# One-core hybrid decoder trunk: the layer norm's steps reordered on VectorE and ScalarE, its third output block staggered further, the last gate block moved to other PSUM banks, the first tile's scores put off

## The chip, the cores and the metric

One core of a Trainium2 chip runs the whole program. The metric is the device time of one execution in microseconds, as the median of several runs. TensorE (PE) does the matmuls, VectorE (DVE), ScalarE (ACT) and GpSimd (POOL) the elementwise work, and SyncE (SP) issues most DMAs. Each engine works through its own queue in order, and engines wait for one another through semaphores.

## What is computed

Two layers over a stream of 1024 positions by 1024 channels: a convolution branch and then an attention branch, each followed by a gated embedding.

```python
# layer 0
h = rms_norm(x, norm_g[0]);  a, b, gate = split(h @ w_in, 3)
y = a * sigmoid(b)
y = depthwise_conv(y, dw) + dw_b                      # 31 taps, causal
y = layer_norm(y, ln_g, ln_b)                         # over the 1024 channels
x = x + (silu(y) * silu(gate)) @ w_out
# after each layer i
gate = sigmoid(rms_norm(x, ple_norm_g[i]) @ ple_w_gate[i])
x = x + (p[i] @ ple_w_proj[i]) * gate
# layer 1
h = rms_norm(x, norm_g[1])
q, k, v, gate = split(h @ attn_w_in, ...)             # 3 dilation groups, 8 heads each, 64 wide
q, k = rope(rms_norm(q)), rope(rms_norm(k))
o = softmax-weighted sum over the groups of banded attention(q, k, v)
x = x + (o * silu(gate)) @ attn_w_out
```

## The kernel before

Channels lie on the 128 partitions, in 8 blocks n of 128; positions lie along the free dimension, in two halves h of 512. A matrix product keeps about float32 precision by splitting both operands into a high part (a rounded copy, made on ACT by `hi_of`) and a low part (the rest, made by `lo_of` on DVE or POOL); each block of products is three matmuls, high by high, high by low and low by high. `weights` (L240) queues a weight block's load, its high part and its low part; the load's target, `raw`, has two buffers.

**The order is written out by hand.** `Order.at(t, fn)` notes a step with a planned time, and `run` issues all steps sorted by it. Planned times set only the order in each engine's queue; they are not waited for. The layer norm's plan is in `Q['ln']`, counted from U, the time planned for its first step.

**The layer norm** (L609 to L676). For each half: `center` (L618) subtracts the mean, which PE has summed into PSUM, from the 8 blocks on DVE, and ACT squares them; `add` (L625) sums the squares, blocks 1 to 3 on POOL and 5 to 7 on DVE; `stat1` (L629) sums over the partitions on PE; `first1` and `step1` (L637, L640) form the reciprocal root (a table load, Ln and Exp on ACT, then four DVE steps); and for each block `yn` (multiply on DVE, SiLU on ACT), `yg` (multiply by the gate on POOL), `ya` (high part on ACT) and `yb` (low part on DVE). Beside it PE computes the last gate blocks (`gacc`, L597 to L606); `gate` multiplies such a block on DVE out of PSUM and takes SiLU on ACT, which needs another table than Ln and Exp. The low parts of the last gate weights and of the first three output weights `w_o` are in the same queues.

**The output product** (L693 to L714). Its first three blocks run together as the halves' channel blocks k become ready: `step_o(n, h, k)` is three matmuls. Blocks 0 and 1 take k at once, block 2 two steps later, and never before U + 30. The other five blocks follow one at a time, then eight embedding blocks `gacc2` (L790 to L827), each evicted by `ple`: a multiply on DVE out of PSUM (L780), a sigmoid on ACT (L781), a multiply and an add. The product's PSUM tiles come in turn from two buffers tagged `mm`; the tile `t` comes from eight buffers tagged `X`, and the result is stored by a DMA from ACT's queue.

**The start of attention** (L1303 to L1362). Attention runs over 48 tiles of 128 positions; each has 24 steps c of two projection matmuls on PE, and `STAGES` (L78) says at which step of which later tile each of a tile's other stages is issued. `turn` transposes q and k on PE, `khi` and `qhi` make their high parts on ACT, `klo` and `qlo` the low parts on DVE; `klo` also issues the DMAs that copy the key parts across partitions in `ring`; `score` is on PE, `top` on DVE, `exp` on ACT. The projected and roped `qs` has one buffer, which the square of the next tile takes as well. The first two tiles share their weights' arrival: tile 1's first half of steps runs inside tile 0, and the stages of both are held back.

Of the kernel before, what the change touches and what calls it, by code (L numbers as in the profile page):

```python
# [58 lines left out]
    rf=-0.1,  # L59

    ln=dict(
        cen=([0.62 * n for n in range(8)], [6.9, 7.5, 8.2, 9.9, 10.5, 15.6, 16.2, 16.8]),
        add=(5, 17.5),
        st=(8, 20.5),
        r1=(9.8, 22.4),
        r2=(11.6, 24.4),
        yn=([14.2, 14.9, 19.5, 20.2, 21, 23, 23.6, 27.2], [26 + 0.7 * n for n in range(8)]),
    ),
)
WKB = 18  # L70
# [17 lines left out]
    11: ((2, "score 0"), (2, "score 1"), (3, "values 0"), (2, "top 0"), (3, "cross 0"),),  # L88
    12: ((2, "top 1"), (2, "exp 0"),),
    15: ((3, "values 1"),),  # L90
    18: ((1, "turn"), (1, "qhi"), (1, "khi"),),
    19: ((3, "store 0"),),
    20: ((1, "klo"), (2, "exp 1"), (3, "cross 1"),),
    22: ((1, "qlo"), (3, "store 1"),),
# [22 lines left out]
class Order:  # L117
# [5 lines left out]
    def at(self, t, fn):  # L123
        self.ops.append((t, len(self.ops), fn))
# [8 lines left out]
def kernel(ctx: ExitStack, tc: tile.TileContext, a, out):  # L133
# [106 lines left out]
    def weights(o, wp, src, nk, t, eng=None, hi=None, lo=None):  # L240

        w = {}
        o.at(t - 30, lambda: w_dma(wp, w, src, nk))
        o.at(t - 14 if hi is None else hi, lambda: w_hi(wp, w, nk))
        o.at(t - (10 if eng is dve else 13) if lo is None else lo, lambda: w_lo(wp, w, nk, eng or pool))
        return w
# [72 lines left out]
    def mm(name):  # L319
        return ps.tile([P, S], F32, name=name, tag="mm", bufs=2)  # L320
# [273 lines left out]
    T_c += Q['mean']  # L594
    U = T_c + Q['cen']
    for n in range(KT):
        wg = weights(o, wp, a["w_cin"][16 + n], KT, T_g + C * n, (pool, dve)[Q['wge'][n]],  # L597
                     lo={5: T_g + C * n - 0.15, 6: U + 6.7, 7: U + 6.8}.get(n))
        te, gacc = chunk(o, T_g + C * n, lambda: mm("gacc"), wg, hh, hl, KT)

        def gate(n=n, gacc=gacc):
            gates[n] = G("gate")
            dve.tensor_mul(gates[n], gacc["a"], rb0)
            act.activation(gates[n], gates[n], AF.Silu)
        at(U + Q['ln']['r1'][0] + 0.05 if n == 5 else te + (0.3 if n == 7 else Q['gt']), gate)

# [32 lines left out]
        rstd_step([sv["rb"][:, halves[h]]], [sv["rt"][:, halves[h]]], [sv["xm", h]])  # L641

    L = Q['ln']
    at(U + 7.4, lambda: act.preload_act_table_set("natural_log_exp_and_others"))
    for h in range(2):
        for n in range(KT):
            at(U + L['cen'][h][n], lambda n=n, h=h: center(n, h))
            if n % 4:
                at(U + (L['add'][h] + 0.65 * (n - 5) if n > 3 else L['cen'][h][n] + 0.1), lambda n=n, h=h: add(n, h))
        at(U + L['st'][h], lambda h=h: stat1(h))  # L650
        at(U + L['r1'][h], lambda h=h: first1(h))
        at(U + L['r2'][h], lambda h=h: step1(h))
    yh, yl, ready = [None] * KT, [None] * KT, [[], []]
    tg = 0
    for h, n in [(0, n) for n in range(7)] + [(1, 0), (1, 1), (0, 7)] + [(1, n) for n in range(2, KT)]:
        def yn(n=n, h=h):
            d = dch[n][:, halves[h]]
            dve.tensor_mul(d, d, sv["rb"][:, halves[h]])
            act.activation(d, d, AF.Silu, scale=vec[:, V_LNG, n : n + 1], bias=vec[:, V_LNB, n : n + 1])

        def yg(n=n, h=h):
            d = dch[n][:, halves[h]]
            pool.tensor_mul(d, d, gates[n][:, halves[h]])

        def ya(n=n, h=h):
            if yh[n] is None:
                yh[n] = H("yhi")
            hi_of(yh[n][:, halves[h]], dch[n][:, halves[h]])

        def yb(n=n, h=h):  # L670
            if yl[n] is None:
                yl[n] = H("ylo")
            lo_of(yl[n][:, halves[h]], dch[n][:, halves[h]], yh[n][:, halves[h]])
        ty = U + L['yn'][h][n]
        tg = max(ty + 1.4, T_g + C * (n + 1) + 1.5 if n == 7 and not h else 0, tg + 1.6)
        at(ty, yn)  # L676
        at(tg, yg)
        at(tg + 1.7, ya)
        at(tg + 3.4, yb)
        ready[h].append(tg + 4.2)  # L680
# [6 lines left out]
    def reopen():  # L687
# [2 lines left out]
        late["gp"] = tc.alloc_tile_pool(name="gp2", bufs=1, side="right", reuse_waits="tile")  # L690
    at(ready[1][-1] + Q['rf'], reopen)

    w_o = [weights(o, wp, a["w_cout"][n], KT, T_o + 8 * n, (pool, dve, dve)[n], U + (9.7, 19, 28.5)[n], U + (9.95, 19.4, 29.5)[n])  # L693
           for n in range(3)]
    acc_o = [{}, {}, {}]

    def open_o():
# [7 lines left out]
                      stop=k == KT - 1 and ww is w["l"])  # L705
    at(T_o - 0.1, open_o)
    for h in range(2):
        for k in range(KT + 2):
            for n in range(3):
                kk = k - 2 if n == 2 else k  # L710
                if 0 <= kk < KT:
                    T_o = max(T_o, ready[h][kk], U + 30 if n == 2 else 0)
                    at(T_o, lambda n=n, h=h, kk=kk: step_o(n, h, kk))
                    T_o += 0.7  # L714
    for n in range(KT):
# [70 lines left out]

    h2h, h2l = [None] * KT, [None] * KT
    at(T_e + 7.5, lambda: ple_stat(lambda: half("ssb2"), X, s2))
    s3 = {}
    ends = []  # L790
    for n in range(KT):
        tn = T_e + C * n + (1.8 if n else 0)
        w = weights(o, wp, a["w_pg"][0, n], KT, tn)
        te, acc = chunk(o, tn, lambda: mm("gacc2"), w, gh, gl, KT)

        def ev1(n=n, acc=acc, what=0):
            s3["t", n] = ple(n, acc["a"], X, s2, halves if n == 7 else whole, s3.get(("t", n)), 5, what)
# [499 lines left out]
    for c in range(24 * (NT - 1) + max(place.values()) + 1):  # L1297
# [24 lines left out]
        for lag, st in STAGES.get(c % 24, ()):  # L1322
            if 0 <= i - lag < NT:
                nm, *pr = st.split()
                held.append((c if i != 1 else max(36, c) if c < 40 else c + 9, getattr(tiles[i - lag], nm), pr))
        for t, fn, pr in [h for h in held if h[0] <= c]:
            fn(*map(int, pr))
        held = [h for h in held if h[0] > c]
# [266 lines left out]
```

## Time and profile before

| | us |
|---|---|
| median of 3 runs | 1317.41 (1316.56 to 1320.78) |
| the profiled execution | 1321.62 |
| its span, first to last instruction | 1319.8 |
| PE busy | 1259.9 |
| DVE, ACT, POOL busy | 999.0, 702.1, 628.1 |

In a timeline row the first number is the start from the beginning of the span, the second the duration; rows of one kind that follow each other are merged (x2, x8). What stands in brackets is how long the engine had idled and what it had waited for. "busy" of merged matmuls includes their overlap: a matmul of 512 columns starts every 0.23 us at the full clock.

### The profile page before, as it was taken

The page shows a single profiled execution, that of the slowest core. Times are in us where ns is not written, and L with a number is a line of the kernel's source. Part 1 is how long each engine was busy: PE and PEld are TensorE (multiplying, and loading weights), DVE is VectorE, ACT ScalarE, POOL GpSimd, SP SyncE. Part 2 cuts the span into 40 slices and gives each one's busy share as a digit, 9 for nine tenths or more (in the row PEclk, how much of TensorE's full clock was granted, in tenths as well). Part 3 has the DMA queues.
Part 4 walks back from the last instruction along what each step waited for, and adds up shares of the span by engine and source line. Part 5 has one row for each costly group of instructions (what it writes and reads, how often), then busy time and mean ns, then how long its engine had stood idle before and what let it go on. Part 6 is the DMA issues. An engine that isn't in the chain of part 4 may idle for free.

```text
span 1319.8 us, 18998 instructions
## 1 busy us (share of the span) xinstructions
PE 1259.9 (95%) x6432; PEld 1043.9 (79%) x6432; DVE 999.0 (76%) x2038; ACT 702.1 (53%) x1552; POOL 628.1 (48%) x742
## 2 busy tenths in 40 slices
PE   7999899999599999899999899999999999999998
PEld 5778788877388788779888799788887888768786
DVE  6899989999948444647987977988878888764522
ACT  6555564556633334645765755655655656424411
POOL 2679899996515355022422622423324424246342
PEclk9999999999799999989999899999999999999999
DMA  7124131113114444601311311411213312117453
GB/s 282 49 99 156 48 128 33 65 32 112 47 50 154 165 176 159 201 17 41 112 61 36 114 56 25 120 25 40 58 47 96 116 30 66 53 50 269 164 203 128
DMA packets 50933, 128.13 MB, mean 97 GB/s; under 512 B 6252, under 2 KB 19764, under 8 KB 50836
## 3 DMA queue, kind: packets, MB, share of 16 engines
q1 hardware_dynamic: 47380, 114.33, 26.7%
q10 hardware_dynamic: 3456, 12.58, 2.5%
q8 instruction: 51, 0.84, 0.3%
q14 instruction: 46, 0.38, 0.1%
HBM read 84.75 MB, written 27.46 MB: 85 GB/s over the span
## 4 chain that ended last, share of the span: by engine, by line
PE 72%; DVE 10%; issue 6%; POOL 6%; ACT 4%; DMA 2%; SPq 0%; POOLq 0%; DVEq 0%; ACTq 0%
PE gacc L183 16%; PE pqk L998 14%; PE oacc L183 8%; PE pv L999 7%; PE bacc L183 5%; PE aacc L183 3%; PE pacc L358 3%; PE oacc L704 2%; POOL wkl L173 2%; PE po L1144 2%; PE tp L1058 2%; PE tq L1126 2%; DVE eA L578 1%; DVE oB L578 1%; PE gacc L1257 1%
## 5 line engine op out<-in xcount | busy, mean ns | idle before, releaser
L998 PE MATMUL pqk<-wkh,h2n 128*128 128x512 f32 x512 | 203.1, 409 | 0.0
L561 POOL TENSOR_TENSOR cc<-cc,tt 128x512 f32<-128x512 f32 x118 | 167.0, 1415 | 21.3 <-ACT tt L560 14.4
L1028 POOL TENSOR_TENSOR fh<-fh 128x8 f32<-128x8 f32 x48 | 9.9, 205 | 290.8 <-ACT fh L1024 286.4
L999 PE MATMUL pv<-wkh,h2n 128*128 128x256 f32 x512 | 144.5, 282 | 0.0
L173 POOL TENSOR_TENSOR wl<-raw,wh 128x1024 fp32r<-128x1024 f32 (+1 forms) x39 | 90.5, 2321 | 70.9 <-ACT wh L167 70.9
L560 ACT ACTIVATE tt<-eo,dws 128x512 f32<-128x512 f32 x118 | 83.4, 721 | 72.9 <-POOL cc L561 72.8
L998 PEld LDWEIGHTS pqk<-wkh,h2n 128*128 128x128 f32 x512 | 98.5, 192 | 19.0 <-issue 2.4
L1120 ACT ACTIVATE pt<-pt,stt 128x128 f32<-128x128 f32 (+1 forms) x192 | 85.1, 444 | 45.5 <-DVE stt L1112 44.0
L998 PE MATMUL pqk<-wkl,h2n 128*128 128x512 f32 x256 | 104.7, 409 | 0.0
L999 PEld LDWEIGHTS pv<-wkh,h2n 128*128 128x128 f32 x512 | 98.8, 193 | 0.0
L578 DVE SCALAR_TENSOR_TENSOR eA<-ypad,dw,eA 128x513 f32<-128x513 f32 x120 | 89.5, 746 | 0.0
L173 DVE TENSOR_TENSOR ring<-tp,ring 64x256 fp32r<-64x256 f32 x96 | 40.5, 422 | 53.7 <-ACT ring L167 50.3
L578 DVE SCALAR_TENSOR_TENSOR oB<-ypad,dw,oB 128x512 f32<-128x512 f32 x104 | 77.5, 745 | 0.0
L1150 ACT COPY ot<-po 64x128 f32<-64x128 f32 x192 | 49.1, 256 | 52.1 <-PE po L1144 50.7
L999 PE MATMUL pv<-wkl,h2n 128*128 128x256 f32 x256 | 72.1, 282 | 0.0
L781 ACT ACTIVATE pt<-pt 128x1024 f32<-128x1024 f32 (+2 forms) x19 | 17.5, 925 | 98.7 <-DVE pt L780 98.7
L167 ACT ACTIVATE wh<-raw 128x1024 fp32r<-128x1024 f32 (+1 forms) x51 | 50.9, 997 | 35.0 <-PE oacc L704 17.9
L780 DVE TENSOR_TENSOR pt<-gacc,rb 128x1024 f32<-128x1024 f32 (+2 forms) x19 | 19.9, 1055 | 64.2 <-PE gacc L183 57.7
L167 ACT ACTIVATE qq<-tp 64x256 fp32r<-64x256 f32 x96 | 36.3, 378 | 53.6 <-PE tp L1058 53.0
L173 POOL TENSOR_TENSOR wkl<-raww,wkh 128x768 fp32r<-128x768 f32 (+1 forms) x24 | 42.5, 1781 | 41.0 <-ACT wkh L167 38.2
L784 POOL TENSOR_TENSOR pt<-pt,xi 128x1024 f32<-128x1024 f32 x12 | 28.9, 2405 | 68.5 <-DVE pt L783 43.1
L1160 DVE TENSOR_TENSOR og<-po,ot 64x128 f32<-64x128 f32 x192 | 54.6, 284 | 6.0
(302 smaller groups left out, 3909.0 us busy)
## 6 DMA issues: line engine op xcount, KB each, us to landing
raww<-in_w_ain_dram SPq DMA_DIRECT2D x48, 384.0 KB
ring<-ring SPq DMA_DIRECT2D x96, 128.0 KB
raw<-in_w_cin_dram SPq DMA_DIRECT2D x22, 512.0 KB
proj_d<-pout SPq DMA_DIRECT2D x16, 512.0 KB
x_d<-x ACTq DMA_DIRECT2D x16, 512.0 KB
raw<-in_w_pg_dram SPq DMA_DIRECT2D x16, 512.0 KB
pj<-proj_d SPq DMA_DIRECT2D x16, 512.0 KB
xi<-x_d SPq DMA_DIRECT2D x16, 512.0 KB
```

Of the source, the lines that this page charges most:

```text
L167: act.activation(hi, src, AF.Copy)
L173: (eng or dve).tensor_sub(lo, src, f(hi))
L183: pe.matmul(dst, w_[:, k, :], x[k][:, sl], start=(k == 0 and i == 0 and j == 0), stop=(k == nk - 1 and i == 1))
L358: pe.matmul(acc[:, sl], q[w, k][:, c], q[x, k][:, sl], start=(k == 0 and ii == 0 and j == 0), stop=(k == 1 and ii == 1))
L560: act.activation(tt, src, AF.Copy, scale=w)
L561: pool.tensor_add(sv["c", n], sv["c", n], tt)
L578: dve.scalar_tensor_tensor(acc, src, w, acc, op0=ALU.mult, op1=ALU.add)
L998: pe.matmul(self.pqk, x, ww[:, :512], start=a0, stop=a1)
L999: pe.matmul(self.pv, x, ww[:, 512:], start=a0, stop=a1)
L1120: act.activation(x, x, AF.Exp, scale=-1.0, bias=nm, accum_out=den)
L1150: act.copy(t[h * HD : h * HD + HD], self.po[pr][HD - h * HD : P - h * HD, h, 0])
L1160: dve.tensor_add(tok(self.u.og[pr][pp[h]], self.g, self.s), *(runs(x, self.g) for x in (self.po[pr][pp[0], h, 1], self.ot[pr][pp[h]])))
```

## The change

In the layer norm, the first half's eight blocks are now finished ahead of the second half's: the second half's centring, its sums, `stat1`, `first1`, `step1` and all of its `yn` are issued later, and block 7 of the first half no longer stands between blocks of the second. The low part of gate weight 6 goes ahead of the layer norm on POOL, that of gate weight 7 from POOL to DVE; gates 5, 6 and 7 and the three output weights get other places. Output block 2 runs five steps behind blocks 0 and 1 in the first half and level with them in the second, without the bound of U + 30. The last embedding block (`gacc2`, n = 7) takes the PSUM tile `eA` in place of an `mm` buffer, and its result tile is `rb0`, which is free by then, in place of an `X` buffer. In attention `khi` is issued ahead of `qhi` for every tile, and the stages `score`, `top` and `exp` of tile 0 are issued 8 steps later.

```diff
     ln=dict(
-        cen=([0.62 * n for n in range(8)], [6.9, 7.5, 8.2, 9.9, 10.5, 15.6, 16.2, 16.8]),
-        add=(5, 17.5),
-        st=(8, 20.5),
-        r1=(9.8, 22.4),
-        r2=(11.6, 24.4),
-        yn=([14.2, 14.9, 19.5, 20.2, 21, 23, 23.6, 27.2], [26 + 0.7 * n for n in range(8)]),
+        cen=([0.62 * n for n in range(8)], [6.9, 7.5, 9.5, 17.0, 18.2, 20.6, 22.0, 23.0]),
+        add=((5, 5.65, 6.3), (23.4, 24.5, 25.1)),
+        st=(6.6, 27.5),
+        tab=7.2,
+        r1=(10.2, 29.6),
+        r2=(12.2, 31.8),
+        yn=([14.6, 15.2, 15.8, 16.4, 17.6, 20.0, 21.4, 28.2], [34.2 + 0.7 * n for n in range(8)]),
+        gate={5: 11.0, 6: 19.0, 7: 27.9},
+
+        wg={6: (-0.5, 0), 7: (8.2, 1)},
+        wo=((8.6, 9.7, 0), (22.5, 26.2, 1), (28, 30.5, 1)),
     ),
@@
-    18: ((1, "turn"), (1, "qhi"), (1, "khi"),),
+    18: ((1, "turn"), (1, "khi"), (1, "qhi"),),
@@
-        wg = weights(o, wp, a["w_cin"][16 + n], KT, T_g + C * n, (pool, dve)[Q['wge'][n]],
-                     lo={5: T_g + C * n - 0.15, 6: U + 6.7, 7: U + 6.8}.get(n))
+        lo, eng = (U + Q['ln']['wg'][n][0], Q['ln']['wg'][n][1]) if n > 5 else (U - 5 if n == 5 else None, Q['wge'][n])
+        wg = weights(o, wp, a["w_cin"][16 + n], KT, T_g + C * n, (pool, dve)[eng], lo=lo)
@@
-        at(U + Q['ln']['r1'][0] + 0.05 if n == 5 else te + (0.3 if n == 7 else Q['gt']), gate)
+        at(U + Q['ln']['gate'][n] if n > 4 else te + Q['gt'], gate)
@@
-    at(U + 7.4, lambda: act.preload_act_table_set("natural_log_exp_and_others"))
+    at(U + L['tab'], lambda: act.preload_act_table_set("natural_log_exp_and_others"))
@@
-                at(U + (L['add'][h] + 0.65 * (n - 5) if n > 3 else L['cen'][h][n] + 0.1), lambda n=n, h=h: add(n, h))
+                at(U + (L['add'][h][n - 5] if n > 3 else L['cen'][h][n] + 0.1), lambda n=n, h=h: add(n, h))
@@
-    for h, n in [(0, n) for n in range(7)] + [(1, 0), (1, 1), (0, 7)] + [(1, n) for n in range(2, KT)]:
+    for h, n in itertools.product(range(2), range(KT)):
@@
-    w_o = [weights(o, wp, a["w_cout"][n], KT, T_o + 8 * n, (pool, dve, dve)[n], U + (9.7, 19, 28.5)[n], U + (9.95, 19.4, 29.5)[n])
-           for n in range(3)]
+    w_o = [weights(o, wp, a["w_cout"][n], KT, T_o + 8 * n, (pool, dve)[e], U + hi, U + lo)
+           for n, (hi, lo, e) in enumerate(L['wo'])]
@@
-        for k in range(KT + 2):
+        lag = 0 if h else 5
+        for k in range(KT + lag):
             for n in range(3):
-                kk = k - 2 if n == 2 else k
+                kk = k - lag if n == 2 else k
                 if 0 <= kk < KT:
-                    T_o = max(T_o, ready[h][kk], U + 30 if n == 2 else 0)
+                    T_o = max(T_o, ready[h][kk])
@@
-    s3 = {}
-    ends = []
+    s3 = {("t", 7): rb0}
@@
-        te, acc = chunk(o, tn, lambda: mm("gacc2"), w, gh, gl, KT)
+        te, acc = chunk(o, tn, (lambda: mm("gacc2")) if n < 7 else (lambda: ps.tile([P, S], F32, name="gacc2b", tag="eA", bufs=1)),
+                        w, gh, gl, KT)
@@
-                held.append((c if i != 1 else max(36, c) if c < 40 else c + 9, getattr(tiles[i - lag], nm), pr))
+                held.append((c + 8 if i == lag == 2 else c if i != 1 else max(36, c) if c < 40 else c + 9, getattr(tiles[i - lag], nm), pr))
```

## Rows read from the trace of the kernel before

**Rows 1.** PE's waits over the span: us in total, times, longest.
```profile
PE tp L1058 <- POOL qs L1052: 8.8, 12, 1.4
PE sc L1097 <- DMA ring<-ring: 3.7, 2, 2.6
```

**Rows 2.** Timeline of PE in the layer norm: start, duration, instruction, [idle before].
```profile
338.86 0.40 PE L704 MATMUL oacc<-yhi,wh 128*128 128x512 f32 x1
...
356.10 0.80 PE L704 MATMUL oacc<-yhi,wh 128*128 128x512 f32 x1 [12.73 <-ACT wh L167]
...
359.05 0.80 PE L704 MATMUL oacc<-yhi,wl 128*128 128x512 f32 x1 [1.73 <-DVE wl L173]
```

**Rows 3.** Chain that ended last, in order of time: start, length, what.
```profile
359.05 31.86 PE oacc L704 x124
...
530.79 9.06 DMA x_d<-pt
...
586.78 0.95 PE sc L1097 x8
```

**Rows 4.** Stretches: length, busy time per engine, granted clock, DMA share, GB/s.
```profile
348.00:365.00 17.00, 7.17 (x16) 5.25 (x17) 17.00 (x14) 10.08 (x15) 13.61 (x8) 0.50 0.18 62
...
542.00:546.00 4.00, 4.00 (x15) 3.42 (x14) 3.36 (x6) 2.37 (x4) 0.00 (x0) 0.57 0.73 263
...
573.00:580.00 7.00, 6.29 (x21) 5.38 (x22) 2.26 (x11) 0.88 (x4) 1.46 (x4) 0.51 0.07 19
```

**Rows 5.** Timeline of DVE in the layer norm.
```profile
295.05 3.65 DVE L557 SCALAR_TENSOR_TENSOR cc<-eo,dws,cc 128x512 f32<-128x512 f32 x2 [0.66 <-POOL cc L561]
...
300.12 0.69 DVE L586 TENSOR_TENSOR d<-cc,Bs 128x512 f32<-128x512 f32 x1
...
302.93 4.88 DVE L619 SCALAR_TENSOR_TENSOR d<-mb,d 128x512 f32<-128x512 f32 x8 [0.98 <-PE mb L612]
...
308.78 4.14 DVE L627 TENSOR_TENSOR sq<-sq,sq 128x512 f32<-128x512 f32 x2 [0.38 <-ACT sq L623]
...
371.60 1.21 DVE L173 TENSOR_TENSOR w<-raw,w 128x1024 fp32r<-128x1024 f32 x1
```

**Rows 6.** Timeline of POOL in the layer norm.
```profile
294.98 2.39 POOL L173 TENSOR_TENSOR wl<-raw,wh 128x1024 fp32r<-128x1024 f32 x1
304.97 1.30 POOL L627 TENSOR_TENSOR sq<-sq 128x512 f32<-128x512 f32 x1 [7.60 <-ACT sq L623]
...
309.53 5.62 POOL L173 TENSOR_TENSOR wl<-raw,wh 128x1024 fp32r<-128x1024 f32 x2
```

**Rows 7.** Groups of POOL from 340 to 372: busy, mean ns, idle before.
```profile
L663 POOL TENSOR_TENSOR d<-d,gate 128x512 f32<-128x512 f32 x12 | 20.4, 1722 | 8.3 <-ACT d L659 5.4 <-ACT gate L604 2.8
```

**Rows 8.** Timeline of ACT at a change of tables in the layer norm.
```profile
341.17 1.28 ACT L659 ACT_TABLE_LOAD   x1
342.46 1.52 ACT L659 ACTIVATE d<-d,vec 128x512 f32<-128x512 f32 x2
```

**Rows 9.** Timeline of PE, DVE and ACT around the last embedding block.
```profile
541.38 0.47 PE L998 MATMUL pqk<-wkh,h2hi 128*128 128x512 f32 x1 [3.15 <-ACT pt L781]
...
544.69 0.84 ACT L167 ACTIVATE wkh<-raww 128x768 fp32r<-128x768 f32 x1 [1.33 <-DMA raww<-in_w_ain_dram]
...
548.88 0.95 DVE L173 TENSOR_TENSOR wkl<-raww,wkh 128x768 fp32r<-128x768 f32 x1
...
551.21 1.82 DVE L173 TENSOR_TENSOR wkl<-raww,wkh 128x768 fp32r<-128x768 f32 x2
...
554.27 1.88 PE L195 MATMUL ssb<-ss,cst 128*128 128x512 f32 x4
```

**Rows 10.** Timeline of ACT, PE and POOL at the first tile's scores.
```profile
568.09 0.60 ACT L1003 ACTIVATE sq<-pqk 128x512 f32<-128x512 f32 x1 [5.19 <-PE tp L1058]
...
573.29 0.55 PE L1099 MATMUL sc<-ring,qq 128*128 128x256 f32 x1 [2.48 <-DVE qs L1041]
...
574.41 0.45 POOL L1052 TENSOR_TENSOR qs<-rt 128x128 f32<-128x128 f32 x1
```

## Prediction, made blind

> **What bounds the kernel now.** I read the busy times first. PE is busy 1259.9 of 1319.8 us, DVE 999.0, so the program is bound by TensorE nearly throughout, and only PE's idle stretches can be won. PE's waits and its timeline say where they are: many short ones behind POOL and the ring DMA [rows 1], and one of 12.73 us behind an ACT step in the layer norm [rows 2]. There PE issues its first output matmul at 338.86, stops after 18 of 144, restarts at 356.10 and stops again until 359.05; from there the chain runs on PE alone for 124 matmuls, to 390.91 [rows 2, 3]. Over 348 to 365 the granted clock is 0.50, the lower of the two levels (1.2 GHz) [rows 4]; matmuls that start every 0.233 us otherwise start every 0.43. Some 21 are slowed, which costs 4.1 us. So this place loses 12.7 + 1.7 + 4.1 = 18.5 us, and nothing else is nearly as large.
>
> Why PE stops: output block 2 stands two steps behind blocks 0 and 1 in PE's queue, and its weight's high part stands late in ACT's. ACT is not full. It waits for DVE, and DVE for POOL. A DVE step with two SBUF operands and a POOL step exclude each other here: a step that takes 0.69 us alone took 2.07 as the mean of two beside POOL's weight splits, the first tap of two lasted until POOL's split ended [rows 5, 6], and POOL's half steps, 1.30 us alone [rows 6], average 1.72 beside DVE's [rows 7]. Steps that read PSUM don't wait: eight centrings take 4.88 us, 0.61 each, although POOL was adding beside them [rows 5]. The last DVE step of the layer norm ends as the next begins, at 371.6 [rows 5].
>
> **The layer norm.** No arithmetic goes; one weight split moves from POOL (2.39 us, [rows 6]) to DVE (1.2 us, as [rows 5], last row). So I walked DVE, ACT, POOL and PE in the new order: each step starts when its engine and inputs are free, 0.60 us for a DVE half step (1.14 for a whole block), 0.5 to 0.8 for ACT halves, 1.30 and 2.39 for POOL, DVE and POOL exclusive where both operands are in SBUF, so that one of each in turn takes 1.7 us. The same walk over the old order restarts PE at 357.2 and 360.1 (trace 356.10 and 359.05 [rows 2]) and ends DVE at 372.6 (371.6): about 1 us late everywhere. Its stations in the new order:
> - POOL now has the split of gate weight 6 straight behind that of weight 5. The second of the two taps of [rows 5] waits for it, 297.8 to 300.6 (2.1 us lost). But the first centring waited 0.98 us for PE anyway [rows 5], so it starts at 303.6 instead of 302.93.
> - The sums no longer meet POOL's two splits; the first half's root is ready at 321.5, where the same walk has 325.8 for the old order.
> - DVE then takes the first half's blocks and, between them, the second half's centrings. The second half's last sum ends at 340.0, where the walk has 332.0 for the old order. PE's `stat1` waits for it, and all output matmuls are queued behind that: PE idles 2.3 us and begins them at 340.9.
> - The first half's 24 steps of 0.70 us last to 357.7. Block 2 is first asked for after 12 of them, at 349.3; its low weight is ready at 346.8. That is where the 12.7 us go. The last low part of this half is ready at 352.05, just when it is asked for.
> - What is late next is the second half: its root (table load, Ln, Exp on ACT, four DVE steps) ends at 351.3, and its first low part only behind seven DVE multiplies that take turns with POOL at 1.7 us: between 360.1 and 362.2, by whether the reload of the SiLU table comes after DVE's first multiply or before it. PE idles 2.2 to 4.4 us, then 1.1 more for the second block, then has 24 steps of 0.70 = 16.8 us.
> - End 378.0 to 380.1 at the full clock. Idle stretches of 3.15 and 2.48 us were each followed by the half clock [rows 4, 9, 10], so I add up to 3.1 us (7 us as in the last row of [rows 4], less than half lost, part of it in place of the 1.1). I take **381.0**, a gain of 390.9 - 381.0 = **9.9 us**, between 8.7 (382.2) and 12.9 (378.0).
>
> Cover: DVE's last layer norm step ends near 370, ten us before PE needs the next weight; after that PE works without a gap to 538.2 (541.38 - 3.15, [rows 9]), and all of it moves up together; a weight late after all would cost its DVE split, 1.2 us [rows 5], or its load. SP's loads keep their places in the plan and hang on freed `raw` buffers; the splits of gate weights 6 and 7 free them at 300.1 and 313.8 in the walk, not at 315.2 at the latest [rows 6], so no output weight lands later.
>
> The second half's chain holds two table loads, and [rows 8] price one: 1.28 us, with the next activation 0.01 us behind it. The Trainium skill (ScalarE: Activation LUTs, What ACT_TABLE_LOAD costs) puts a drain of about 1.38 us on top of every load; by that the product would end 2.8 us later. These rows show no drain, and the sum goes without it.
>
> **The last embedding block.** In the old order PE ends `gacc2` near 538.2 and idles 3.15 us [rows 9]: the first projection's banks are those of the last block's `mm` buffer, and DVE evicts it late because its result tile waits for a store's DMA that took 9.06 us [rows 3]. `eA` and `rb0` remove both waits. PE goes on at 538.2 and keeps its clock (rows of 0.57 granted from 542 to 546 [rows 4]: eight steps at 0.57 us instead of 0.353, 1.8 us). Those 4.9 us are not kept. Step 28 needs the low part of weight row 5, ready at 549.8, and step 31 that of row 6, at 552.2 [rows 9]; row 5 waits for its DMA, which landed at 544.6 whatever PE did [rows 9]. At 0.353 us a step PE is there at 548.1, waits 1.7, then 1.3, and starts `ssb` at about 552.3 instead of 554.27. Gain **2.0 us**; bounds 0 (SP's queue, which isn't ordered by hand, gives the loads other places) and 4.9 (loads earlier too).
>
> **The first tile's scores.** PE waited 2.48 us for `qlo`, 0.4 for the DMA, and ran at half clock until 580 [rows 4, 10]. Eight steps later is 8 x 0.353 = 2.8 us of matmuls in that place. What is late next is tile 1's `turn`, at step 66 now ahead of the scores: its chain starts when tile 0's `turn` frees `qs` (ACT's square at 568.09) and ends with POOL's rope at 574.86 [rows 10]; with `khi` first DVE's `klo` and `qlo` are out of the way 0.8 us earlier, so 574.6, and PE is there at 573.3: a wait of 1.4 us. The scores follow, 575.4 to 576.4. Tile 0's second `exp` now stands behind the first's high part on ACT and holds PE another 0.5 us at step 77; tile 1's ring copy, now behind four DVE `top` steps, lands at 581.9, 1 us before it is asked for. Tile 1's scores then start at 583.0 instead of 586.78 [rows 3]. Gain **3.8 us**; bounds 1 (clock falls for 6.8 us all the same, 3 us) and 5.5 (the turn doesn't wait).
>
> **`khi` ahead of `qhi`, all other tiles.** The two orders take ACT equally long, and DVE's `klo`, the ring copy and the score can each come 0.77 us (two copies of 0.38) earlier. PE's two longest ring waits sum to 3.7 us [rows 1]: at most 1.5 comes back there and about as much in shorter ones; but 8.8 us of waits for POOL's rope stand right beside them [rows 1], and a PE that arrives earlier waits longer there. I take **1.0**, between 0 and 3.
>
> **Sum.** 9.9 + 2.0 + 3.8 + 1.0 = 16.7 us. The profiled execution took 1321.62 (span 1319.8 and 1.8 around it), so 1304.9 in its own time; the median of the runs stands 4.2 lower at 1317.41, so **1300.7, call it 1301**.
>
> **The rivals.**
> - *Only the layer norm pays.* The weight loads eat the whole head start of the attention stage, and the delayed scores only move the wait to `turn` with the half clock behind it: 9.9 + 1.0 of gain, 1306.5. For it: the loads' DMA share was 0.73 at 542 to 546 [rows 4]. Against: the walk leaves two thirds of the score gain with a margin at each station. 0.17.
> - *All of it.* The clock holds in the layer norm (378.0), the loads move up, the turn doesn't wait: 12.9 + 4.9 + 5.5 + 1 = 24 us, 1293. It needs every bound at once; half of the way is likelier. 0.08.
> - *No change.* SP's order is not written by hand; if the changed program's loads of output weights or projection weights come a position later, behind a transfer that waits, PE stands for the 9 us of such a transfer [rows 3] at one or two places: 1310 to 1319. 0.07.
> - *Slower: the second half starves PE.* All second-half work is now behind the first half's on DVE. PE has 16.8 us of first-half matmuls to hide it, from 340.9. If `stat1` or the root comes later than in my walk by x, PE ends x later. The other gains spent as well (6.8), it decides against the change from x = 16.7; with x = 22, as if 20 DVE steps each met a POOL multiply (1.1 us each), 1323. The old order has DVE meet POOL all the way from 343 to 367 already [rows 7], so this is unlikely. 0.03.
> - *A change of tables costs twice its load.* If ACT stood for a second 1.28 us at each of the two loads between the second half's sum and its first low part, PE's stop there would be 2.6 us longer: 1303.3, inside the forecast's own range. The 0.01 us in [rows 8] speaks against it. 0.05. (It is the drain that the Trainium skill names, at a price from the rows.)
>
> **How the numbers follow.** The forecast, 1296 to 1305.5, has 0.60; with the rivals that is 1. The range runs from 1294 to 1310: it leaves out half of the case that all pays, and what lies beyond the no-change case's near edge and the slow one, under 0.2. A measurement of this kernel can tell about 0.3% (4 us) from no change: faster than 1313.5 are the forecast, the tables, the first two rivals and part of the third, 0.93; within it 0.04; slower 0.03.
>
> **What would show it right or wrong.** PE's timeline should have its first L704 matmul near 341 after some 2 us of idle time for DVE's sum, no wait for `wh` or `wl`, one stop of 2 to 5 us near 358 to 362 for `ylo`, and the output product at 381, ten us earlier. The first projection should follow `gacc2` with no idle time, with short waits for `wkl` ten us on. Tile 1's `turn` should wait 1 to 2 us for POOL and the first scores for nothing. The forecast is wrong if PE stops for longer than 6 us at the second half, if weights of the output product arrive late, or if the half clock stays for more than 7 us at a place.

## The result, and the profile after

| | us | against before, with 95% interval |
|---|---|---|
| predicted | 1301 (1294 to 1310) | |
| before, median beside it | 1318.89 (1316.56 to 1320.78) | |
| **after, median** | **1307.38** (1307.03 to 1309.46) | 0.9918 (0.9901 to 0.9934) |
| after, timed a second time | 1308.26 (1305.00 to 1309.51) | 0.9924 (0.9906 to 0.9941) |
| profiled execution: before, after, after a second time | 1321.62, 1307.48, 1305.00 | |

The change saves 11.5 us: inside the range, but 6.4 us above the forecast, and outside the 1296 to 1305.5 to which the text gave 0.60. PE is busy 1257.4 of 1305.7 us.

To see where, I take the start of six matmuls in the two traces and compare what lies between them. Six stretches, each beginning where the last one ends, cover before's span from 174 to 1141 us; the 179 us behind them are equally long in both traces:

1. *Layer norm and output blocks 0 to 2*: from the last `pacc` matmul (173.93 in before) to the first matmul of output block 3;
2. *Output weight 5*: from there to the first matmul on the low part of output weight 5;
3. *Rest of layer 0*: from there to the last embedding block's last matmul;
4. *First projection*: from there to the first tile's statistics (`ms`);
5. *First scores*: from there to the fourth `tq` (the first tile's probabilities, transposed);
6. *Attention*: from there to the last `tq`.

| length, us | 1 | 2 | 3 | 4 | 5 | 6 |
|---|---|---|---|---|---|---|
| before | 216.81 | 23.33 | 123.75 | 18.25 | 28.32 | 556.54 |
| after | 208.24 | 24.27 | 123.86 | 16.25 | 24.26 | 556.67 |
| after, second profile | 207.90 | 24.28 | 123.86 | 16.04 | 23.04 | 555.80 |
| first profile less before | -8.57 | +0.94 | +0.11 | -2.00 | -4.06 | +0.13 |

The stretches sum to -13.45; 0.68 lie ahead of the first, in the wait for the first load.

PE's timeline of the changed kernel, at the places that answer to [rows 2], [rows 9] and [rows 10]:

```profile
341.14 2.08 PE L637 MATMUL ssb<-sq,cst 128*128 128x512 f32 x2 [3.29 <-DVE sq L632]
342.23 1.42 PE L709 MATMUL oacc<-yhi,wh 128*128 128x512 f32 x1
...
363.53 0.50 PE L709 MATMUL oacc<-ylo,wh 128*128 128x512 f32 x1 [1.41 <-DVE ylo L178]
...
366.92 0.50 PE L709 MATMUL oacc<-ylo,wh 128*128 128x512 f32 x1 [1.02 <-DVE ylo L178]
...
405.76 0.50 PE L188 MATMUL oacc<-yhi,wl 128*128 128x512 f32 x1 [0.77 <-POOL wl L178]
...
529.85 0.40 PE L1004 MATMUL pqk<-wkh,h2hi 128*128 128x512 f32 x1
...
533.52 0.50 PE L1004 MATMUL pqk<-wkl,h2hi 128*128 128x512 f32 x1 [1.05 <-DVE wkl L178]
...
564.71 0.66 PE L1064 MATMUL tp<-cst,qs 128*128 128x128 f32 x4 [1.62 <-POOL qs L1058]
...
565.56 0.64 PE L1105 MATMUL sc<-ring,qq 128*128 128x256 f32 x4
```

The 12.73 us are gone; PE stops for DVE's sum ahead of the product and twice briefly for the second half's low parts. The projection starts without a wait, the scores too. Besides the 1.62 us ahead of `turn`, three waits are new: weight 5's low part at 405.76, and projection weights at 533.52 and (1.04 us, not shown) 543.60.

The stretches of [rows 4] in the changed kernel (length, busy time per engine, granted clock, DMA share, GB/s), and one ahead of them:

```profile
340.00:348.00 8.00, 6.86 (x16) 4.74 (x17) 7.48 (x10) 4.00 (x6) 0.62 (x1) 0.57 0.17 66
348.00:365.00 17.00, 15.59 (x67) 12.26 (x66) 14.95 (x14) 10.21 (x14) 11.32 (x8) 1.00 0.21 62
542.00:546.00 4.00, 2.96 (x12) 1.36 (x11) 3.14 (x5) 1.44 (x2) 0.00 (x0) 1.00 0.75 246
573.00:580.00 7.00, 7.00 (x48) 6.34 (x46) 4.31 (x17) 4.59 (x17) 1.48 (x4) 1.00 0.01 4
```

The half clock has left all three places of before. It now stands right behind the 3.29 us stop, where PE still has its stop at 363 ahead of it and loses little. Over the whole span below 1200 us the granted clock is 0.5 for 41.0 us in before's trace, 23.9 in after's and 13.7 in its second profile.

### The profile page after: what moved, and what is told of

It is laid out like the page before. It is cut to its first block, busy times and chain, and to the rows that moved or that the text cites. A ratio compares the mean times of both kernels' runs of the same rounds, so it can differ in the third digit from the quotient of the medians.

```text
span 1305.7 us, 19028 instructions
## 1 busy us (share of the span) xinstructions
PE 1257.4 (96%) x6432; PEld 1041.1 (80%) x6432; DVE 997.6 (76%) x2039; ACT 696.6 (53%) x1552; POOL 626.1 (48%) x741
## 4 chain that ended last, share of the span: by engine, by line
PE 57%; DVE 16%; POOL 12%; issue 9%; ACT 5%; DMA 1%; POOLq 0%; SPq 0%; ACTq 0%; DVEq 0%
PE pqk L1004 13%; PE gacc L188 12%; PE pv L1005 7%; PE oacc L188 6%; POOL cc L566 4%; PE bacc L188 3%; DVE eA L583 2%; DVE oB L583 2%; POOL wkl L178 2%; PE po L1150 2%; PE tp L1064 2%; PE pacc L363 1%; PE tq L1132 1%; PE gacc L1263 1%; DVE d L663 1%
## 5 line engine op out<-in xcount | busy, mean ns | idle before, releaser
L172 ACT ACTIVATE ring<-tp 64x256 fp32r<-64x256 f32 x96 | 36.2, 377 | 55.6 <-PE tp L1064 54.6
```

The source lines that it names most:

```text
L172: act.activation(hi, src, AF.Copy)
```

## Experiments: the layer norm

**Lag or order?** My text put the end of the 12.7 us down to block 2's lag of five steps. The rival is the order on DVE and ACT. The two were taken apart.

The old kernel with the new lag alone:

```diff
-        for k in range(KT + 2):
+        lag = 0 if h else 5
+        for k in range(KT + lag):
...
-                kk = k - 2 if n == 2 else k
+                kk = k - lag if n == 2 else k
...
-                    T_o = max(T_o, ready[h][kk], U + 30 if n == 2 else 0)
+                    T_o = max(T_o, ready[h][kk])
```

> The old order on VectorE and ScalarE with the new lag alone (third output block five steps late in the first half, level with the others in the second, no due time of its own). Theory 'order' (the third block's weight stands late in ScalarE's queue behind work of the layer norm, and a step five later still comes before it): the stop of 12.73 us stays, cut only by the three steps of blocks 0 and 1 that now stand ahead of it (6 steps of 0.70 us, taken out of later places); the output product ends between 389 and 393 us of the span, within 2 us of the kernel before, and the whole is within 0.3% of it. Theory 'lag' (the prediction's sentence that block 2 is first asked for later, 'that is where the 12.7 us go'): the stop shrinks by most of its length, the product ends near 380 to 383, and the whole is 8 to 10 us faster than before.

Measured: 1320.16 us, ratio 1.0014 (0.9998 to 1.0030). Stretch 1 is 218.11, 1.3 longer than before. PE's timeline, its waits from 341 to 366:

```profile
342.17 0.51 PE L704 MATMUL oacc<-yhi,wh 128*128 128x512 f32 x1 [1.21 <-ACT yhi L167]
344.67 0.50 PE L704 MATMUL oacc<-ylo,wh 128*128 128x512 f32 x1 [2.00 <-DVE ylo L173]
...
349.83 0.79 PE L704 MATMUL oacc<-ylo,wh 128*128 128x512 f32 x1 [2.95 <-DVE ylo L173]
...
356.69 0.50 PE L704 MATMUL oacc<-yhi,wl 128*128 128x512 f32 x1 [0.67 <-DVE wl L173]
...
360.06 0.79 PE L704 MATMUL oacc<-ylo,wh 128*128 128x512 f32 x1 [2.62 <-DVE ylo L173]
...
365.71 0.79 PE L704 MATMUL oacc<-ylo,wh 128*128 128x512 f32 x1 [1.30 <-DVE ylo L173]
```

The long stop is gone, and nothing is won. Where PE no longer asks for the weight, it asks for high and low parts that aren't there: six stops of 10.75 us in sum, 8.87 of them for `ylo`, and 20.5 us of half clock among them (17.1 in before). The wait for `wh` had stood in front of others that cost as much once the half clock is counted; the row [rows 2] names the first only. Theory "lag" falls. Of theory "order" the times hold (the product ends at 389.66), but not its way there: it expected the 12.73 us to stay.

The whole change with the old lag:

```diff
-        lag = 0 if h else 5
+        lag = 2
```

> The whole change but with the old lag of two steps in both halves. Theory 'order': the output product ends 0 to 2 us later than in the changed kernel (381.5 of the span), because block 2's low weight (about 347) is waited for 2 to 3 us at its first step, in the shadow of the wait for the second half; the 0.77 us wait for the low part of the next weight but two (seen at 405.76 in the changed kernel) goes, as block 0 ends 1.4 us earlier against the end of the product. Whole: within 1 us of the changed kernel. Theory 'lag': the stop of some 10 us comes back and the whole is within 3 us of the kernel before.

Measured: 1306.94 us, ratio 0.9911 (0.9884 to 0.9938). Stretch 1 is 208.89, up to 1 us over the changed kernel; stretch 2 is 23.33, 0.94 under it. As expected but for the wait at block 2's first step: there is none. PE comes to that weight only at 349.8, after matmuls at half clock, and DVE ends its low part at 349.3. So the lag has no part in the gain: it gives 0.6 to 1.0 us in stretch 1 and takes 0.94 in stretch 2. "Order" stands here for all else that the diff moves in the layer norm, weights and gates included, and for the bound of U + 30 that is gone; no run takes these apart.

**The wait that the lag makes.** With no lag in the second half, block 0's last step lies two steps (1.4 us) before the end of the product instead of four (2.8 us). The evictions follow, behind them on DVE the rotary angles, and on ACT weight 5's high part stands behind the sine of those angles. ACT and POOL in the changed kernel:

```profile
401.22 0.37 ACT L418 ACTIVATE rope<-rope 128x192 f32<-128x192 f32 x1 [7.31 <-DVE rope L417]
401.91 0.36 ACT L421 ACTIVATE rope<-rope 128x192 f32<-128x192 f32 x1 [0.32 <-DVE rope L420]
402.18 1.04 ACT L172 ACTIVATE wh<-raw 128x1024 fp32r<-128x1024 f32 x1
```
```profile
403.30 2.41 POOL L178 TENSOR_TENSOR wl<-raw,wh 128x1024 fp32r<-128x1024 f32 x1 [6.76 <-ACT wh L172]
```

POOL ends at 405.71 and PE starts at 405.76; the run with the lag alone has the same wait, 0.76 us. If that is the chain, the angles put behind the weight end it:

```diff
         if n == 2:
-            at(te + 5, rope)
+            at(te + 9, rope)
```

> The changed kernel with the angles of the rotary embedding planned four units later, so that ScalarE splits output weight 5 before it waits for VectorE's angles. Theory: the 0.77 us wait of PE for POOL's low part of that weight at 405.76 goes (PE reaches that matmul 0.8 to 1.1 us earlier against the end of the output product's first three blocks) and nothing else changes: 0.5 to 1.1 us less at the first projection. Rival (POOL's split is late for another reason, its raw load or POOL's own queue): the wait stays between 0.5 and 1 us.

Measured: 1306.63 us, ratio 0.9912 (0.9879 to 0.9945). POOL starts that split at 398.53, PE doesn't wait for it, and stretch 2 is 23.33 as in before. The cause is shown; of the total, 0.8 us can't be told from its spread.

**What bounds the layer norm now.** DVE waits for the second half's root behind the first half's work (changed kernel):

```profile
349.95 0.69 DVE L220 TENSOR_TENSOR rt<-rb 128x512 f32<-128x512 f32 x1 [2.08 <-ACT rb L214]
...
353.07 8.71 DVE L663 TENSOR_TENSOR d<-d,rb 128x512 f32<-128x512 f32 x7
361.71 1.76 DVE L178 TENSOR_TENSOR ylo<-d,yhi 128x512 fp32r<-128x512 f32 x1
```

So I put the second half's root ahead, and its last two multiplies between the low parts:

```diff
-        st=(6.6, 27.5),
+        st=(6.6, 26.45),
-        r1=(10.2, 29.6),
-        r2=(12.2, 31.8),
-        yn=([14.6, 15.2, 15.8, 16.4, 17.6, 20.0, 21.4, 28.2], [34.2 + 0.7 * n for n in range(8)]),
+        r1=(10.2, 26.5),
+        r2=(12.2, 28.05),
+        yn=([14.6, 15.2, 15.8, 16.4, 17.6, 20.0, 21.4, 28.2], [31.0 + 0.7 * n for n in range(6)] + [36.0, 37.6]),
```

> The changed kernel with the second half's root and multiplies put three units earlier and its last two multiplies between the low parts. Theory (the second half's chain on VectorE is what PE waits for in the layer norm, 1.41 and 1.02 us at 363 to 367): the root starts right behind the second half's sum, the first low part of the second half comes 3 us earlier, PE's two waits go, and the output product ends 2.4 to 2.9 us earlier than in the changed kernel; of that up to 1 us is lost again at the low part of output weight 5. Rival (VectorE and POOL exclude each other, so that moving work earlier only delays the first half's last parts): PE waits as long, now for the first half's low parts or block 2's weight, and the product ends within 1 us of the changed kernel's or later.

Measured: 1305.20 us, ratio 0.9894 (0.9873 to 0.9915). Stretch 1 is 205.01, 2.9 to 3.2 under the changed kernel. DVE's root and first low part, then PE's only wait for the second half's parts:

```profile
345.40 0.69 DVE L220 TENSOR_TENSOR rt<-rb 128x512 f32<-128x512 f32 x1
...
359.99 1.78 DVE L178 TENSOR_TENSOR ylo<-d,yhi 128x512 fp32r<-128x512 f32 x1
```
```profile
361.82 0.50 PE L709 MATMUL oacc<-ylo,wh 128*128 128x512 f32 x1 [0.65 <-DVE ylo L178]
```

The root comes 4.6 us earlier and without a wait; the first low part only 1.7 us earlier. The first half's last multiply, one more of its low parts and the split of output weight 2 now stand behind the root, and from 354.88 on DVE's steps still take 1.78 us each beside POOL. But the second low part is there at 364.06, just as PE asks for it.

## Experiments: the last embedding block

The change but for this part:

```diff
-    s3 = {("t", 7): rb0}
+    s3 = {}
...
-        te, acc = chunk(o, tn, (lambda: mm("gacc2")) if n < 7 else (lambda: ps.tile([P, S], F32, name="gacc2b", tag="eA", bufs=1)),
+        te, acc = chunk(o, tn, lambda: mm("gacc2"),
```

> The changed kernel with the last embedding block back in the common banks and in a fresh result tile. Theory (the prediction's): before the first projection PE waits about 3 us for the eviction of the last block, as in the kernel before (3.15); the two short waits for the projection weights' low parts (1.05 and 1.04 us, at the seventh and the 31st step) get shorter or go, since PE comes later to the same weights; at the first tile's statistics the kernel is 1.6 to 2.0 us later than the changed one. Rival 'loads move up': the weights' low parts also come later by the 3 us and the whole is 3 to 5 us later. Rival 'nothing': within 0.5 us.

> The last embedding block back in the common banks and a fresh result tile, timed for longer. In its trace PE waits 1.49 us ahead of the first projection, and one of the two waits of 1 us for the projection weights' low parts is gone for it, so that PE is level again at the first tile's statistics. Theory 'worth nothing, the weights take it back': median within 1 us of the changed kernel timed beside it. The prediction's theory: 2.0 us above it.

Measured: 1308.24 and 1308.92 us, ratios 0.9918 (0.9902 to 0.9935) and 0.9932 (0.9915 to 0.9949); 0.9 above the changed kernel in the first and 0.7 above it, on the same chip, in the second. Stretch 4 is 16.55 and 16.97. In the eight profiles with the edit and otherwise the same projection it is 15.77 to 16.56, 16.26 in the mean. So undoing the edit costs about 0.5 us there, not 2.0. DVE's eviction of the last block in before and in the run with the lag alone, which has the old arrangement too, then in the two undo runs, and PE's first projection matmul in the second of these:

```profile
539.94 1.29 DVE L780 TENSOR_TENSOR pt<-gacc,rb 128x512 f32<-128x512 f32 x2 [1.87 <-DMA x_d<-pt]
```
```profile
538.80 1.29 DVE L781 TENSOR_TENSOR pt<-gacc,rb 128x512 f32<-128x512 f32 x2 [0.79 <-DMA x_d<-pt]
```
```profile
530.39 1.29 DVE L786 TENSOR_TENSOR pt<-gacc,rb 128x512 f32<-128x512 f32 x2 [0.20 <-PE gacc L188]
```
```profile
531.64 0.69 DVE L786 TENSOR_TENSOR pt<-gacc,rb 128x512 f32<-128x512 f32 x1 [0.55 <-DMA x_d<-pt]
```
```profile
533.08 0.47 PE L1004 MATMUL pqk<-wkh,h2hi 128*128 128x512 f32 x1 [1.85 <-ACT pt L787]
```

The store for which DVE stood 1.87 us in before holds it for 0 and 0.55 here, so PE waits 1.49 and 1.85 instead of 3.15 [rows 9]; and the weight at 533.52 takes most of that back (its wait is gone in both runs). In the run with the lag alone DVE stands 0.79 us, PE waits 2.08 and stretch 4 is 17.14, so before's 1.87 isn't a fixed price of the old arrangement. Why the store lands sooner in the others, the runs don't say.

## Experiments: the first scores, and `khi` ahead of `qhi`

The change without the eight steps:

```diff
-                held.append((c + 8 if i == lag == 2 else c if i != 1 else max(36, c) if c < 40 else c + 9, getattr(tiles[i - lag], nm), pr))
+                held.append((c if i != 1 else max(36, c) if c < 40 else c + 9, getattr(tiles[i - lag], nm), pr))
```

> The changed kernel with the first tile's scores issued where the kernel before has them (no eight steps of hold). Theory (the prediction's): PE waits 2 to 2.6 us for the first score's query part and falls to the half clock for some 7 us; the first tiles' scores and what follows come 3.8 to 4.3 us later than in the changed kernel, measured at the second tile's projections and at the third tile. Rival (the wait for the rotary step at the second tile's turn only moves; nothing is won): within 1 us of the changed kernel at the third tile.

Measured: 1310.87 us (1308.20 to 1314.00), ratio 0.9949 (0.9931 to 0.9966): 3.5 us above the changed kernel, and 3.9 to 4.2 above the two kernels that were timed beside it on the same chip (1306.94 and 1306.63). The profiled execution is the shortest of its eight; in it stretch 5 is 25.78, 1.5 over the changed kernel. PE's two waits and the clock there:

```profile
564.11 0.36 PE L1105 MATMUL sc<-ring,qq 128*128 128x256 f32 x1 [2.60 <-DMA ring<-ring]
565.00 0.59 PE L1105 MATMUL sc<-ring,qq 128*128 128x256 f32 x3 [0.53 <-DMA ring<-ring]
```
```profile
563.00:570.00 7.00, 5.36 (x32) 4.69 (x33) 2.92 (x13) 2.28 (x8) 1.70 (x5) 1.00 0.13 32
```

The wait stands where [rows 10] has it and is as long, now behind the ring's DMA, but the full clock stayed. So by this trace the hold is worth the wait alone, 1.5 us and not the 3.8 to 4.3 expected; by the median it is worth 3.5. That the other 2 are half clock, which this execution escaped, agrees with the granted clocks of all executions: 0.9896 in the mean of these eight, 0.9925 in that of the eight of the two kernels beside it. At which place the others ran slower isn't shown.

The swap undone:

```diff
-    18: ((1, "turn"), (1, "khi"), (1, "qhi"),),
+    18: ((1, "turn"), (1, "qhi"), (1, "khi"),),
```

> The changed kernel with the query part copied before the key part again. Theory 'readers of one tile wait in program order' (VectorE's first low part starts behind all four ScalarE copies of the transposed tile in either order): 0 us, within 0.5 us at the last tile and within 1.5 us in the median; VectorE's wait behind ScalarE's last copy stays at about 0.84 us a tile. The prediction's theory: ring copies 0.77 us later in each tile, and 1.0 us (0 to 3) slower over the whole; first tile's turn for tile 1 waits about 0.8 us longer (2.4 instead of 1.62).

> The query part copied before the key part again, timed for longer. Measured before this run: 3.4 us above the changed kernel in the median, but in its trace VectorE's key low part starts 1.65 us after the transposes in the median tile, and in the changed kernel 1.64. Theory 'no effect, the 3.4 us are where the half clock fell': median within 1.5 us of the changed kernel timed beside it. Theory 'the swap is worth 1 to 3 us' (the prediction's term was 1.0): median 1.5 to 3.5 us above it.

Measured: 1310.73 us first, 0.9936 (0.9919 to 0.9954); then 1307.90, 0.9926 (0.9910 to 0.9942), beside 1308.26 for the changed kernel on the same chip. Stretch 5 is 0.29 and 0.27 longer than in the changed kernel's two profiles, stretch 6 1.65 and 0.68 longer; the second of the two (556.48) lies within the spread of the kernels that have the new order of copies (555.0 to 557.1), the first (558.32) doesn't. PE's idle time in stretch 6 doesn't differ: 19.5 to 21.9 us in the four profiles with the old order, 19.8 to 21.8 in the nine with the new. DVE's first low part starts 1.65 us after the tile's transposes in the median of 48 tiles, in either undo run; in the changed kernel 1.64. One tile of the changed kernel, ACT and then DVE:

```profile
867.20 0.78 ACT L172 ACTIVATE ring<-tp 64x256 fp32r<-64x256 f32 x2 [0.75 <-PE tp L1064]
868.00 0.77 ACT L172 ACTIVATE qq<-tp 64x256 fp32r<-64x256 f32 x2
```
```profile
868.81 0.88 DVE L178 TENSOR_TENSOR ring<-tp,ring 64x256 fp32r<-64x256 f32 x2 [0.84 <-ACT qq L172]
```

The key copies are done at 867.98, but DVE's `klo` waits for the query copies as well. My reading is that engines that read one PSUM tile, here `tp`, take turns in program order; then the order of ACT's copies can't move `klo`. The swap is worth 0.3 us at the first tile, and more isn't shown. The Trainium skill (PSUM — Partial Sum Buffer, PSUM bank collisions raise a hardware error) says that two engines may not read one bank at once in the same partitions, and that software must keep them apart; the 0.84 us for which DVE stands here agree.

If this is so, `klo` between the copies starts earlier:

```diff
-    18: ((1, "turn"), (1, "khi"), (1, "qhi"),),
+    18: ((1, "turn"), (1, "khi"),),
...
-    20: ((1, "klo"), (2, "exp 1"), (3, "cross 1"),),
+    20: ((1, "klo"), (1, "qhi"), (2, "exp 1"), (3, "cross 1"),),
```

> The changed kernel with the key part's two VectorE steps put between the key copies and the query copies (key copies, key low parts, query copies, query low parts). Theory 'readers of one tile wait in program order': VectorE starts the key's low part right behind the second ScalarE copy, 0.75 us earlier in each tile, and the ring's DMA is issued 0.7 us earlier; PE's waits for the ring's DMA (4.8 us after the 550th us in the changed kernel, five of them) shrink by 1 to 3 us, part of it given back at the query's low part, which is 0 to 0.5 us later; whole 0 to 2 us faster. Rival (VectorE was held by something else): VectorE's low part starts where it did, and the query parts come 0.8 us later: 0 to 2 us slower.

Measured: 1334.42 us, ratio 1.0118 (1.0100 to 1.0136), 27 us slower. The mechanism holds: DVE's low part starts 0.85 us after the transposes, and PE's waits for the ring's DMA after 550 fall from 4.8 to 0.6 us (6.8 in the changed kernel's second profile). That the shared tile is what held DVE, and not all that ACT had been given before, isn't tested. The price was missed. ACT's groups (busy, mean ns, idle before them), the query copies in the changed kernel and in this one, then PE's waits in this one:

```profile
L172 ACT ACTIVATE qq<-tp 64x256 fp32r<-64x256 f32 x96 | 36.4, 379 | 1.8
```
```profile
L172 ACT ACTIVATE qq<-tp 64x256 fp32r<-64x256 f32 x96 | 36.5, 380 | 64.7 <-DVE ring L178 64.1
```
```profile
PE tp L1064 <- POOL qs L1058: 18.0, 23, 2.5
PE po L1150 <- DVE pp L178: 9.3, 12, 1.7
PE tq L1132 <- ACT pt L1126: 8.1, 14, 1.9
```

ACT now stands 1.3 us a tile for DVE, with all its later work behind it: PE's waits for `qs` double, and waits for ACT's `pt` appear that the changed kernel hasn't (0.07 us).

## A version that is faster than both

> The changed kernel unaltered, timed once more so that the two undo runs beside it have the same chip and the same number of rounds to be set against. Both theories: 1307 us within 1.5, and the stretches of half clock at other places than in the first profile, by up to two of 3.4 us more or less.

Measured: 1308.26 us, as expected; between its two profiles the half clock differs by 10.2 us, three such stretches and not up to two.

Three steps on the changed kernel: the earlier second half, the later angles, and the low parts of projection weights ahead of the last block's own steps:

```diff
     ev4(6)
+    los[2]()
     ev1(what=1)
-    los[2]()
...
     hi_k(6)
+    los[5]()
     ev4(7)
     ev2()
-    los[5]()
+    los[6]()
     ev3(7)
-    los[6]()
```

> Three steps on top of the changed kernel: the layer norm's second half earlier (2.4 us less at the first projection by its own run), the angles of the rotary embedding behind the split of output weight 5 (0.8 us less by its own run), and the low parts of projection weights 2, 5 and 6 ahead of the last embedding block's own steps on VectorE. Theory: the first two add up, since they end different waits, and PE's waits of 0.65 to 1 us for weight 5's low part and of 1.05 and 1.04 us for projection weights 2 and 6 go: PE is 4 to 5 us earlier at the first tile's statistics than in the changed kernel, and the whole is 3 to 5 us faster, 1302 to 1304 us. Rival (the weights are late because their loads are, and the last block's own steps are late instead): the waits stay or move to the block's low part, 2.4 to 3.2 us earlier, 1304 to 1305 us.

Measured: 1302.93 us (1299.65 to 1306.24), ratio 0.9890 (0.9871 to 0.9910); 5.3 under the changed kernel timed beside it, whose lowest of six runs is 1305.00; four of these six are below that. Stretches 1, 2 and 4 are 205.31, 23.33 and 14.82: 2.8, 0.9 and 1.3 less than the mean of the changed kernel's two profiles, 5.0 in sum. PE's wait for weight 5 and its two of 1 us for `wkl` are gone; 0.37 us for a `wkl` is left at 532.06, and in the layer norm, behind the 3.29 ahead of `stat1`, this one:

```profile
363.07 0.50 PE L709 MATMUL oacc<-ylo,wh 128*128 128x512 f32 x1 [0.61 <-DVE ylo L178]
```

## Why the prediction came out 6 us low

**The layer norm: right in size, wrong in its reason.** 9.9 forecast, 8.6 and 8.9 measured, by the lower end of 8.7. The stations of the walk against the trace of after:

| station | walk | trace |
|---|---|---|
| first centring | 303.6 | 303.66 |
| first half's root ready | 321.5 | 322.31 |
| second half's last sum | 340.0 | 341.09 |
| PE's first L709, idle before `stat1` | 340.9, 2.3 | 342.23, 3.29 |
| block 2's low weight | 346.8 | 347.86 |
| first half's last low part | 352.05 | 353.15 |
| second half's root | 351.3 | 352.55 |
| its first low part | 360.1 to 362.2 | 363.47 |

The walk keeps within 1.3 us to the end, on durations of before alone; for the last row that is its later case, the one with the table's reload ahead of DVE's first multiply, as the trace has it (350.45 and 353.07). That the product ends at 381.49, so near 381.0, is in part luck: the walk is 1.3 us early there, and the half clock that the text added behind the second half's stop came right behind the first stop, where a shorter wait at 363 (1.41 us, 2.67 in the second profile) took up what it cost. The reason given for the gain failed: it named the lag, because the one long row named the weight. The run with the lag alone wins nothing, the one with the order alone wins all; I had asked the walk about the whole change only. Also, the text counted 21 matmuls slowed in before, 4.1 us; [rows 4] have 16, some 3.2. The sum doesn't use them.

**"PE works without a gap, and all of it moves up together": failed, 0.94 us.** A late weight of the output product stands on the text's own list of signs of being wrong. I looked at DVE's own last step for cover and not at what follows from block 0's end: evictions, angles, sine, then weight 5. Its slack had been small: in before POOL ended that split at 413.58, PE took it at 414.08.

**The last block: the term of 2.0 was mis-sized.** Between the traces stretch 4 shrinks by 2.00, just as forecast, but that is luck: undone, the edit is worth 0.5. The step that failed is the store's 9.06 us [rows 3], taken as fixed; in the chains of the run with the lag alone and of the second undo run it is 7.97 and 7.75. What was right is that the weights take back most of a head start. Of their two waits the text had 1.3 us at step 31, where 1.04 came; its 1.7 at step 28 didn't come, and 1.05 at step 7 wasn't in it.

**The scores: right in the main.** 3.8 forecast; 4.06 and 5.28 between the traces, 3.5 by the undo run's median, of which its trace shows the 1.5 of the wait. Tile 1's `turn` waits 1.62 us (1.4 forecast), the scores wait for nothing.

**`khi`: forecast 1.0, shown 0.3.** The step that failed is that `klo` can come 0.77 us earlier. It waits for ACT's last copy in either order (1.65 us after the transposes, and 1.64).

**The offset of 4.2 us: the largest miss.** In its own time the forecast was 1304.9, and the profiled executions of after took 1307.48 and 1305.00. To reach a median I then took off the 4.2 us by which before's profiled execution exceeded its median. The changed kernel's profiled executions don't exceed theirs: 1307.48 against 1307.38, and 1305.00 against 1308.26. Before's trace has 41.0 us of half clock, 27.3 of them at the three places that the change mends, so part of its excess was counted once in the terms and once in the offset. The granted clocks of before's 35 executions beside the experiments bear out that the excess is clock: the ten shortest took 1315.6 us in the mean at 0.987, the ten longest 1320.6 at 0.983, and 0.004 of 1318 us is about the 5 us between them (an estimate). At which places a shorter execution keeps its clock isn't shown, as no shorter one of before was profiled.

**The rivals.** "Only the layer norm pays" gave 1306.5 and came nearest, for another reason: the scores paid, the last block hardly did. The second half doesn't starve PE. The loads of tables cost what [rows 8] show: ACT's load at 347.32 takes 1.28 us and the next activation starts 0.02 us behind it. The drain of about 1.38 us that the Trainium skill (ScalarE: Activation LUTs, What ACT_TABLE_LOAD costs) adds doesn't show here either.

## What to carry to other kernels

A wait in a trace names the input that came last at that matmul, not the next one; before a stop is put down to one input, ask when the others were ready, here by a walk of every queue over the rows' durations. A difference between two traces at a place isn't the worth of the edit made there; the undo run is. An offset between a profiled run and its median may sit in the very stalls that a change removes, and then it mustn't be taken off again.

## What was not expected of the hardware

- **The half clock doesn't follow every stop of the same length.** PE idled 2.48 us ahead of the first scores in before and went on at half clock [rows 4, 10]; the run without the hold idled 2.60 there and kept 1.00. After the 3.28 to 3.32 us ahead of `stat1`, 3.4 us of half clock came in ten of twelve profiles and 6.8 in two (after and the run without the hold). Stretch 1 hardly differs (208.24 with 6.8 us, 207.90 with 3.4), because PE waits 1.41 us for the second half in the one and 2.67 in the other.
- **One kernel's executions spread by 4.5 us** (1305.00 to 1309.51 for after). Its two profiles, 1307.48 and 1305.00, have 23.9 and 13.7 us of half clock and, behind PE's first matmul, 35.9 and 38.4 us of PE idle time.
- **DVE and POOL took turns at one fixed price**: from 354.88 on in after, four DVE multiplies in a row took 1.78 us each, with a POOL multiply between, where the three ahead of them took 0.68; the walk's 1.7 was near.
